# Split weights in the three standing places: all written 64 bytes further on

## The chip, the cores and the metric

The kernel runs on one core of a Trainium2 chip. The metric is the device time of one execution, in microseconds (us). Matrix products are TensorE's (PE in the profile; PEld is its loading of the operand that stays in the array). VectorE (DVE) and ScalarE (ACT) work element by element, GpSimd (POOL) does very little here, and SyncE (SP) issues nearly all DMAs from the device memory into the on-chip buffer, in which a tile has 128 partitions and a free dimension.

## The reference

Two layers of a diffusion backbone over 256 latent tokens of width 2048, with 256 context tokens, everything in float32. Layer 0 projects with one wide matrix into attention heads (q, k, v, a gate) and into a state-space branch (z, x, B, C, dt); layer 1 is a gated short convolution. Cut to the products that matter:

```python
def na_ssd_mixer(h, hc, w_in, ..., w_out, update_ctx):
    p = h @ w_in                      # q, gate, z, k, v, x, B, C, dt
    pc = hc @ w_in[:, base:]          # context: k, v, x, B, C, dt
    ...
    out = jnp.concatenate([ya, yb], axis=-1) @ w_out

def short_conv_mixer(h, w_in, conv_w, w_out):
    p = h @ w_in
    bg, cg, hv, g = jnp.split(p, 4, axis=-1)
    y = bg * dw_conv(cg * hv, conv_w)
    return (jax.nn.silu(g) * y) @ w_out

def reference(x, c, ctx, c_ctx, ada_w, ada_b, norm_g, ...):
    for i in range(DEPTH):
        shift, scale, gate = adaln(c, ada_w[i], ada_b[i])
        h = modulate(rms_norm(x, norm_g[i]), shift[:, None], scale[:, None])
        ...
        x = x + gate[:, None] * y
    return x
```

## The kernel before

**Products in split form.** A float32 matrix product is made of three products of a reduced type (fp32r). Each factor is split into a high part (the value cast to fp32r) and a low part (the value less its high part), and high x high, high x low and low x high are summed in a bank of the accumulator memory. For the activations these parts stand in tiles hH and hL (or mix, h1, y2 later on).

**How a weight comes in.** The weights are read in 454 chunks of 512 KB. `weight` (L410) puts them into a list in the order of their use. `issue` (L381) starts a DMA on SyncE's queue whenever a raw buffer is free. `split` (L422) takes the next chunk when one of the *places* is free: ScalarE casts it into the high part H (L441), and VectorE subtracts H from the raw chunk into the low part Lo (L448, in `low_part`). `use` (L485) hands H and Lo to the products, and `used` (L498) gives the place back. For the whole of layer 0 there are three standing places, the tiles w0, w1, w2 of 2112 elements a partition (L168). Near the end of the output projection three more are made of tiles that are no longer needed (KL; QT with QL; wH5 with wL5, L425), and they serve in turn with the standing ones for the rest.

**Where in a place.** A chunk has 1024 elements a partition. Most chunks are written to elements 0 to 1023 (H) and 1024 to 2047 (Lo). The chunks of the gates, of z and of C are marked in the set `shifted` when they are listed (L522 to L524), and written 16 elements, that is 64 bytes, further on: 16 to 1039 and 1040 to 2063 (L439). Either way H and Lo lie next to each other. The two dt chunks hold both parts in one half of a place (L431).

**How a product reads a place.** `mm` (L201, its product at L204) multiplies. In `mm_act` (L699) the activations are loaded into the array and 512 columns of H or Lo stream through it: this is how q, k, v, both output projections and the second layer's input are made. In `mm_ws` (L709) 128 columns of H or Lo are loaded and the activations stream: 512 columns wide (latent and context) for B and x, 256 wide (latent only) for the gates, z and C. The opening (`first`, L1086, k-block 0) and the next six blocks (`block`, L981) write these products out in an order and at times set by hand. In the opening `high_terms` (L1225) multiplies with a high part before `low` (L965) and `low_terms` (L1235) deal with its low part.

**What sets the order of the rest.** The program is emitted in one order, and a small planner (`Plan`, L38) keeps a time for every engine while it is emitted. It does so by pieces of tiles: `keys` (L50) maps an operand to units of 128 elements (L55), and for each unit it knows when it was last written and read. From the eighth k-block on, generators for the side work (attention heads, state-space groups, row reductions, output stages) wait in queues. After every few products `pump` (L287) asks `may` (L256) whether the planner's times allow the next step of each, and emits it there. The row reductions of the modulation weights (L842) go by the planner's TensorE clock too (L837). `take` (L190) picks the buffer or bank that the planner saw used longest ago.

Of the kernel before, what the change touches and what calls it, by code (L numbers as in the profile page):

```python
# [17 lines left out]
COL_Q, COL_G, COL_Z, COL_K, COL_V, COL_X = 0, 2048, 4096, 6144, 8192, 10240  # L18
COL_B, COL_C, COL_DT = 12288, 13312, 14336
# [122 lines left out]
def kernel(ctx: ExitStack, tc, x, cx, ada0, w0, adaT, w_in, w_out, sc_in, sc_out, rpb, small, const,  # L142
# [12 lines left out]
    def st(shape, tag, dt=F32, name=None):  # L155
        return sb.tile(list(shape), dt, tag=tag, name=name or tag, bufs=1)
# [9 lines left out]
    free_b = [pj.tile([128, 512], F32, tag=f"bank{k}", name=f"bank{k}", bufs=1) for k in range(8)]  # L166
    free_r = [st([128, 1024], f"raw{k}") for k in range(NRAW)]
    places = [st([128, 2112], f"w{k}", F32R) for k in range(NW)]  # L168
    WH = [t[:, :1024] for t in places]
    WL = [t[:, 1024:2048] for t in places]  # L170
    shifted = set()


    xrow = [st([128, D], "KT", name="x0")]
# [26 lines left out]
    def mm(o, l, r, start, stop):  # L201
        if start:
            bits[o.tensor.name] = o.shape[0] == 128 and o.shape[-1] == 512
        E(T.matmul(o, l, r, start=start, stop=stop, skip_group_check=True))  # L204
# [13 lines left out]
    def spawn(q, gen, tmps=0, halves=0, late=0):  # L218
        q.append(Task(gen, tmps, halves, late))
# [125 lines left out]
    def bank(*full_):  # L345
        if not full_:
            return take(free_b)
        b = min(free_b, key=lambda a: (bits.get(a.tensor.name) is not full_[0], plan.last[a.tensor.name]))
        free_b[:] = [a for a in free_b if a is not b]
        return b  # L350
# [30 lines left out]
    def issue():  # L381

        while (loads or later) and (free_r or (loads and callable(loads[0]))):
            if loads and loads[0] is None:
                if not gate[0]:
                    return
                loads.popleft()
                continue
            if loads and callable(loads[0]):
                loads.popleft()()  # L390
                continue
            if later and (not loads or (ngem[0] < loads[0][7] and len(RAW) - ngem[0] >= 5 - loads[0][7])):
                kind, key, w, r0, nb, c0, n = later.popleft()
                ngem[0] += 1
            elif loads:
                kind, key, w, r0, nb, c0, n, _ = loads.popleft()
            else:
                return
            raw = raw_()
            v = raw[:, :nb * n].rearrange("p (b c) -> p b c", b=nb)  # L400
            if w is ada0 or w is w0 or w is adaT:
                E(DMA.dma_start(raw, w[r0]))
            else:
                E(DMA.dma_start(v, w[r0:r0 + nb * 128, c0:c0 + n].rearrange("(b p) c -> p b c", p=128)))
            RAW[key] = (raw, v)

    nw = [0]
    room = [2]

    def weight(w, r0, nb, c0, n):  # L410
        loads.append(("w", nw[0], w, r0, nb, c0, n, room[0]))
        nw[0] += 1
# [5 lines left out]
    def place():  # L418
        in_use.append(free_w.popleft())
        return in_use[-1]  # L420

    def split():  # L422
        k = pos["split"]
        raw, v = RAW.pop(k)
        nb, n = v.shape[1], v.shape[2]  # L425
        w = place()
        if n == 64:

            while lows:
                low_part()  # L430
            W = WH[w].rearrange("p (b c) -> p b c", b=nb)  # L431
            E(S.copy(W[:, :, :64], v))
            E(V.tensor_tensor(out=W[:, :, 64:], in0=v, in1=W[:, :, :64].bitcast(F32), op=ALU.subtract))
            HL[k] = (W, None)
            pos["split"] += 1
            give_raw(raw)
            issue()
            return
        H, Lo = (places[w][:, 16:1040], places[w][:, 1040:2064]) if k in shifted else (WH[w], WL[w])  # L439
        H, Lo = (t[:, :nb * n].rearrange("p (b c) -> p b c", b=nb) for t in (H, Lo))  # L440
        E(S.copy(H, v))  # L441
        lows.append((k, H, Lo, v, raw))
        pos["split"] += 1

    def low_part():

        k, H, Lo, v, raw = lows.popleft()
        E(V.tensor_tensor(out=Lo, in0=v, in1=H.bitcast(F32), op=ALU.subtract))  # L448
        HL[k] = (H, Lo)
        give_raw(raw)  # L450
        issue()
# [5 lines left out]
    def cast_half(b):  # L457
# [4 lines left out]
        raw, v = RAW[0]  # L462
        E((S.copy, V.tensor_copy)[b](WH[0].rearrange("p (b c) -> p b c", b=2)[:, b], v[:, b]))

    def low_half0(b):

        raw, v = RAW[0]
        H, Lo = (w[0].rearrange("p (b c) -> p b c", b=2) for w in (WH, WL))
        E(V.tensor_tensor(out=Lo[:, b], in0=v[:, b], in1=H[:, b].bitcast(F32), op=ALU.subtract))
# [48 lines left out]
    def q_proj(w, c0, nc_, rows=D):  # L518
        room[0] = 2 if w is w_in and c0 >= COL_K else 1
        nb = 1024 // nc_  # L520
        for r0 in range(0, rows, nb * 128):
            if w is w_in and (COL_G <= c0 < COL_K or COL_C <= c0 < COL_DT):  # L522

                shifted.add(nw[0])  # L524
            weight(w, r0, nb, c0, nc_)

    def give_raw(raw):
        if raw.tensor.name not in once_names and not (started[0] and raw.tensor.name in spare_names):
            free_r.append(raw)
# [80 lines left out]
    for i in (2, 3, 4):  # L610
# [4 lines left out]
    ssd_cols = lambda s: [(w_in, COL_B + s * 256, 256), (w_in, COL_C + s * 256, 256), (w_in, COL_X + s * 512, 512),  # L615
                          (w_in, COL_Z + s * 512, 512)]
    q_proj(w_in, CG(0), 512)
    for r0 in (0, 1024):
        weight(w_in, r0, 8, COL_DT, 64)
    for j_ in ssd_cols(0)[1::2]:  # L620
        q_proj(*j_)
    for a in range(1, 4):
        qk = [(w_in, CQ(a), 512), (w_in, CK(a), 512)]
        gv = [(w_in, CG(a), 512), (w_in, CV(a), 512)][::-1 if a in () else 1]
        for j_ in qk + gv + ssd_cols(a) if a < 3 else qk + ssd_cols(a) + gv:
            q_proj(*j_)
# [333 lines left out]
    def cast(i):  # L960
        if pos["split"] <= i:
            assert pos["split"] == i and free_w and i in RAW, (i, pos, list(free_w), sorted(k for k in RAW if type(k) is int))
            split()
# [122 lines left out]
    def first():  # L1086
# [125 lines left out]
        def k_lat(k, term):  # L1212
            for t in range(2):
                if k == 0 and term == 0:
                    box["K", t] = bank()
                H, Lo = (w[0].rearrange("p (b c) -> p b c", b=2) for w in (WH, WL))
                tt = slice(t * 128, (t + 1) * 128)
# [7 lines left out]
        def high_terms(key, t):  # L1225
            ps = psQ[t] if key == "Q" else bank()
            box[key, t] = ps
            k_ = "KVQ".index(key)
            H = WH[k_].rearrange("p (b c) -> p b c", b=2)
            tt = slice(t * 128, (t + 1) * 128)  # L1230
# [4 lines left out]
        def low_terms(key, t):  # L1235
            k_ = "KVQ".index(key)
            Lo = WL[k_].rearrange("p (b c) -> p b c", b=2)
            tt = slice(t * 128, (t + 1) * 128)
# [45 lines left out]
        def ctx_high(t, k):  # L1284
            tt = slice(t * 128, (t + 1) * 128)
            for key in "KV":
                if k == 0:
                    box[key, t] = bank()
                for w in (WH, WL):
                    mm(box[key, t], hH[k][:, tt], w["KV".index(key)].rearrange("p (b c) -> p b c", b=2)[:, k],  # L1290
# [931 lines left out]
    def turn_gen():  # L2222
        yield when(lambda: n_back[0] >= 11.5 and attn[0] == 32 and ssd_done[0] == 8)
        pt = st([128, 2, 4, 256], "PT", name="late")
        for k in range(2):
            late[4 * k:4 * k + 4] = [pt[:, k, q, :] for q in range(4)]
            pts.append(pt[:, k])
        E(V.scalar_tensor_tensor(out=A1, in0=M1[:, 1], scalar=1.0, in1=P_("g1"), op0=ALU.add, op1=ALU.mult))
        for kp in range(0, KB, 2):
            yield when(lambda: ("x1", kp // 4) in got and (kp < 8 or len(passed) == 4))  # L2230
            yield W_("PE", x1[0][:, kp * 128:(kp + 2) * 128], x1[1][:, kp * 128:(kp + 2) * 128], nb=1)
            pt = bank()
            for b in range(2):
                for t in range(2):
                    turn(pt[:, b * 256 + t * 128:b * 256 + (t + 1) * 128], x1[t][:, (kp + b) * 128:(kp + b + 1) * 128])
            if kp == 14:
                yield when(lambda: ("h1", 7, 0) in got)
            for b in range(2):
                kb = kp + b
                if kp < 8 or kp == 14:  # L2240
                    yield W_("ACT", pt)
                    E(S.activation(late[kb], pt[:, b * 256:(b + 1) * 256], AF.Copy, scale=A1[:, kb:kb + 1]))
                else:

                    held[kb] = pt
                got.add(("turn", kb))
            if kp < 8 or kp == 14:
                give(free_b, pt)
# [131 lines left out]
    for ns in ((0, 512), (1024,), (1536,)):  # L2380
# [41 lines left out]
        if len(ns) == 2:  # L2422
            force(lambda: attn[0] == 32 and not side)
            x1 += [st([128, D], "KT", name="x1a"), st([128, D], "Vt", name="x1b")]
            for H, Lo in ((KL[:, 0:2], KL[:, 2:4]), (QT, QL), (st([128, 4, 256], "gt", F32R, name="wH5"), st([128, 4, 256], "sz", F32R, name="wL5"))):

                free_w.append(len(WH))
                WH.append(H.rearrange("p a b -> p (a b)"))
                WL.append(Lo.rearrange("p a b -> p (a b)"))
            spawn(side, turn_gen())  # L2430
# [106 lines left out]
    for i in range(4):  # L2537
        for part, gen in ((1, cg_gen), (2, hv_gen), (3, gg_gen), (0, bg_gen)):
            ps = banks(2)
            kb0 = 0  # L2540
            if i == 0 and part == 1:
# [3 lines left out]
                for t in range(2):  # L2545
                    for kb in range(8):
# [3 lines left out]
                        H, Lo = ws[kb // 2]  # L2550
# [132 lines left out]
```

## Time and profile before

| | us |
|---|---|
| runs | 1724.03, 1723.19, 1724.82 (median 1724.03) |
| the profiled execution | 1723.43 |
| its span, first to last instruction | 1721.6 |
| TensorE products busy | 1715.5 |
| VectorE busy | 1279.5 |
| ScalarE busy | 823.0 |

A group's line in the profile names the source line, the engine, the operation and the tiles (written <- read, buffer numbers left out), the shape, the count, then the busy time and the mean duration, and the idle time of the engine before it with what ended it. For a product the first tile after the arrow is the one that streams, the second the one that is loaded. Products overlap: each shows about 390 ns for 512 columns, while the next starts well before it ends, so the pace is read from the distance of starts. The granted TensorE clock is 1.00 over the whole span.

### The profile page before, as it was taken

The numbers are of one execution on the slowest core, as the hardware profiler recorded it, in microseconds if no ns is written. First come the engines' busy times: TensorE is split into PE (matmuls) and PEld (weight loads), VectorE is DVE, ScalarE is ACT, GpSimd is POOL, SyncE is SP. The second block draws the span as 40 slices with busy tenths as digits, with TensorE's granted clock in tenths as the row PEclk, the third lists the DMA queues.
The fourth block names the chain that finished last, engine by engine and source line by source line (L and its number), as shares of the span: only waits on it lengthen the run. The fifth ranks groups of instructions, "written<-read, shape, count | busy, mean of one in ns | idle before, by whom it ended". The sixth has DMA issues, their size and how long they took to land.

```text
span 1721.6 us, 24689 instructions
## 1 busy us (share of the span) xinstructions
PE 1715.5 (100%) x9129; PEld 1449.9 (84%) x9129; DVE 1279.5 (74%) x2161; ACT 823.0 (48%) x1450; POOL 34.3 (2%) x28
## 2 busy tenths in 40 slices
PE   9999999999999999999999999999999999999999
PEld 5778899888889889889888898888888888888887
DVE  5699878877886778486877587887667767676754
ACT  6578464434553445244444244655444444444342
POOL 0000010000000000000001000000000000000000
PEclk9999999999999999999999999999999999999999
DMA  9988566456645675754775577767857788787863
GB/s 360 355 293 285 199 195 204 152 178 217 222 144 166 205 230 165 243 173 155 226 227 164 191 214 235 237 214 266 288 190 249 274 270 298 251 288 250 286 213 117
DMA packets 191368, 391.03 MB, mean 227 GB/s; under 512 B 16200, under 2 KB 45960, under 8 KB 190992
## 3 DMA queue, kind: packets, MB, share of 16 engines
q1 hardware_dynamic: 183936, 382.88, 67.2%
q10 hardware_dynamic: 7312, 6.59, 1.2%
q8 instruction: 71, 1.16, 0.3%
q14 instruction: 49, 0.40, 0.1%
HBM read 379.79 MB, written 9.62 MB: 226 GB/s over the span
## 4 chain that ended last, share of the span: by engine, by line
PE 99%; DMA 1%; DVE 0%; issue 0%
PE bank L204 96%; PE bank L209 3%; DMA raw<-in_ada 0%; DMA small<-in_small 0%; DVE tmp L2575 0%; DVE tmp L2578 0%
## 5 line engine op out<-in xcount | busy, mean ns | idle before, releaser
L441 ACT CAST w<-raw 128x1024 fp32r<-128x1024 f32 (+1 forms) x336 | 350.9, 1045 | 477.5 <-PE bank L204 389.2
L448 DVE TENSOR_TENSOR w<-raw,w 128x1024 fp32r<-128x1024 f32 (+1 forms) x336 | 406.9, 1215 | 215.0 <-ACT w L441 212.3
L204 PE MATMUL bank<-hH,w 128*128 128x256 f32 (+1 forms) x2064 | 486.5, 324 | 0.0
L204 PE MATMUL bank<-w,hH 128*128 128x512 f32 x1280 | 402.0, 394 | 0.0
L204 PEld LDWEIGHTS bank<-hH,w 128*128 128x128 f32 x2064 | 345.2, 188 | 32.1 <-issue 1.7
L204 PE MATMUL bank<-hL,w 128*128 128x256 f32 (+1 forms) x1040 | 334.7, 322 | 0.0
L204 PEld LDWEIGHTS bank<-w,hH 128*128 128x128 f32 x1280 | 236.9, 188 | 47.2 <-issue 0.8
L204 PE MATMUL bank<-w,hL 128*128 128x512 f32 x640 | 248.6, 391 | 0.0
L204 PEld LDWEIGHTS bank<-hL,w 128*128 128x128 f32 x1040 | 196.4, 189 | 14.5
L204 PE MATMUL bank<-w,h 128*128 128x512 f32 x768 | 178.5, 390 | 0.0
L204 PEld LDWEIGHTS bank<-w,h 128*128 128x128 f32 x768 | 144.0, 188 | 29.7
L842 DVE CUSTOM_DVE_ANT_0 raw<-raw,csb 128x1024 f32<-128x1024 f32 x128 | 155.3, 1219 | 10.5 <-DMA raw<-in_adaT 10.4
L204 PEld LDWEIGHTS bank<-w,hL 128*128 128x128 f32 x640 | 120.1, 188 | 25.3 <-DVE hL L1123 0.4
L204 PE MATMUL bank<-w,mix 128*128 128x512 f32 x588 | 138.4, 392 | 0.0
L204 PEld LDWEIGHTS bank<-w,mix 128*128 128x128 f32 x588 | 109.5, 188 | 22.0 <-issue 0.2
L204 PE MATMUL bank<-KL,h 128*128 128x512 f32 x264 | 63.6, 389 | 0.0
L1817 DVE SCALAR_TENSOR_TENSOR tmp<-bank,cwh,tmp 128x508 f32<-128x508 f32 (+1 forms) x80 | 59.4, 745 | 1.6
L204 PEld LDWEIGHTS bank<-KL,h 128*128 128x128 f32 x264 | 49.6, 188 | 10.3
L448 DVE TENSOR_TENSOR KL<-raw,KL 128x1024 fp32r<-128x1024 f32 x32 | 39.2, 1224 | 23.5 <-ACT KL L441 23.3
L204 PE MATMUL bank<-QT,h 128*128 128x512 f32 x168 | 55.8, 391 | 0.0
L204 PE MATMUL bank<-wH,h 128*128 128x512 f32 x168 | 55.3, 389 | 0.0
L441 ACT CAST QT<-raw 128x1024 fp32r<-128x1024 f32 x32 | 33.6, 1051 | 41.9 <-PE bank L204 34.5
(343 smaller groups left out, 2077.8 us busy)
## 6 DMA issues: line engine op xcount, KB each, us to landing
raw<-in_w_in SPq DMA_DIRECT2D x188, 512.0 KB, 3.7
raw<-in_adaT SPq DMA_DIRECT2D x128, 512.0 KB, 4.8
raw<-in_sc_in SPq DMA_DIRECT2D x128, 512.0 KB, 4.6
raw<-in_w_out SPq DMA_DIRECT2D x64, 512.0 KB, 4.6
raw<-in_ada SPq DMA_DIRECT2D x39, 512.0 KB, 6.2
raw<-in_sc_out SPq DMA_DIRECT2D x32, 512.0 KB, 4.5
tmp<-dram_csr SPq DMA_DIRECT2D x32, 256.0 KB, 5.8
raw<-in_w SPq DMA_DIRECT2D x15, 512.0 KB, 5.9
```

Source lines behind the costliest of these rows:

```text
L204: E(T.matmul(o, l, r, start=start, stop=stop, skip_group_check=True))
L209: E(T.transpose(o, i, ident if k == 128 else ident[:k, :k]))
L441: E(S.copy(H, v))
L448: E(V.tensor_tensor(out=Lo, in0=v, in1=H.bitcast(F32), op=ALU.subtract))
L842: E(V.tensor_tensor_reduce(out=raw, in0=raw, in1=csb, scale=1.0, scalar=0.0, op0=ALU.mult, op1=ALU.add, accum_out=gp[:, h, m:m + 1]))
L1817: E(V.scalar_tensor_tensor(out=do, in0=di, scalar=cwh[:, 32 * k + ch:32 * k + ch + 1], in1=do, op0=ALU.mult, op1=ALU.add))
```

## The change

The set `shifted` goes, and the views WH and WL of the three standing places themselves begin 16 elements further on. So every chunk that is split into w0, w1 or w2 is written there, the dt chunks and those of the opening too, which use WH and WL directly (`cast_half`, `low_half0`, `high_terms`, `low_terms`, `ctx_high`, `ctx_low`). The three later places, made of other tiles, keep their addresses.

```diff
     places = [st([128, 2112], f"w{k}", F32R) for k in range(NW)]
-    WH = [t[:, :1024] for t in places]
-    WL = [t[:, 1024:2048] for t in places]
-    shifted = set()
+    WH = [t[:, 16:1040] for t in places]
+    WL = [t[:, 1040:2064] for t in places]
...
-        H, Lo = (places[w][:, 16:1040], places[w][:, 1040:2064]) if k in shifted else (WH[w], WL[w])
+        H, Lo = WH[w], WL[w]
         H, Lo = (t[:, :nb * n].rearrange("p (b c) -> p b c", b=nb) for t in (H, Lo))
         E(S.copy(H, v))
...
         for r0 in range(0, rows, nb * 128):
-            if w is w_in and (COL_G <= c0 < COL_K or COL_C <= c0 < COL_DT):
-
-                shifted.add(nw[0])
             weight(w, r0, nb, c0, nc_)
```

## The prediction

> **What bounds the kernel now.** I read the page first: busy times, then the chain that ended last.
>
> ```profile
> span 1721.6 us, 24689 instructions
> PE 1715.5 (100%) x9129; PEld 1449.9 (84%) x9129; DVE 1279.5 (74%) x2161; ACT 823.0 (48%) x1450; POOL 34.3 (2%) x28
> ...
> PE 99%; DMA 1%; DVE 0%; issue 0%
> PE bank L204 96%; PE bank L209 3%; DMA raw<-in_ada 0%; DMA small<-in_small 0%; DVE tmp L2575 0%; DVE tmp L2578 0%
> ```
>
> The chain is TensorE from end to end, 96% of it the product helper at L204. A change that touches no product's pace and makes no product wait cannot move the end. So the questions are two: what a product costs when one of its operands lies 64 bytes further on, and whether the split weights come late anywhere. The second is answered by the view of waits, for the weight loads of TensorE (total us, times, longest):
>
> ```profile
> PEld bank L204 <- issue: 20.1, 70, 0.5
> ...
> PEld bank L204 <- DVE w L448: 0.6, 2, 0.4
> ...
> PEld bank L204 <- ACT w L441: 0.4, 1, 0.4
> ```
>
> In 1,721.6 us, TensorE waited 1.0 us for the two halves of split weights together. The splits have cover to spare.
>
> Which products read the three standing places, and how? In a name like bank<-w,hH the operand that streams through the array stands first and the one that is loaded into it second. The groups of TensorE by shape, over the whole span and, for the last one, over its last 91 us:
>
> ```profile
> L204 PE MATMUL bank<-w,hH 128*128 128x512 f32 x1280 | 402.0, 394 | 0.0
> L204 PE MATMUL bank<-hH,w 128*128 128x512 f32 x784 | 255.1, 394 | 0.0
> L204 PE MATMUL bank<-w,hL 128*128 128x512 f32 x640 | 248.6, 391 | 0.0
> L204 PE MATMUL bank<-hH,w 128*128 128x256 f32 x1280 | 232.8, 282 | 0.0
> L204 PE MATMUL bank<-hL,w 128*128 128x256 f32 x640 | 178.7, 279 | 0.0
> L204 PE MATMUL bank<-w,h 128*128 128x512 f32 x768 | 178.5, 390 | 0.0
> L204 PE MATMUL bank<-hL,w 128*128 128x512 f32 x400 | 156.0, 390 | 0.0
> L204 PE MATMUL bank<-w,mix 128*128 128x512 f32 x588 | 138.4, 392 | 0.0
> ```
>
> ```profile
> L204 PE MATMUL bank<-w,y 128*128 128x512 f32 x180 | 41.7, 390 | 0.0
> ```
>
> The 256-wide products, 1280 + 640 = 1,920, are the gates, z and C: their weights are shifted already and stay where they are. The change reaches two other kinds. **Streamed:** 1280 + 640 + 768 + 588 + 180 = 3,456 products of 512 columns whose moving operand is a split weight (k, v, q, both output projections, the second layer's input). **Loaded:** 784 + 400 = 1,184 products of 512 columns whose weight is the loaded operand (x, B, the two dt chunks).
>
> **Their pace.** The means above include the overlap of neighbours, so the pace is read from starts in the timeline. Four stretches without an interruption (start, duration, group):
>
> ```profile
> 355.01 0.39 PE L204 MATMUL bank<-w,hL 128*128 128x512 f32 x1
> ...
> 358.41 0.39 PE L204 MATMUL bank<-w,hL 128*128 128x512 f32 x1
> ```
>
> ```profile
> 1309.68 4.47 PE L204 MATMUL bank<-w,h 128*128 128x512 f32 x19
> 1313.99 2.88 PE L204 MATMUL bank<-KL,h 128*128 128x512 f32 x12
> 1316.71 0.39 PE L204 MATMUL bank<-QT,h 128*128 128x512 f32 x1
> ```
>
> ```profile
> 541.77 0.28 PE L204 MATMUL bank<-hL,w 128*128 128x256 f32 x1
> ...
> 544.95 0.28 PE L204 MATMUL bank<-hL,w 128*128 128x256 f32 x1
> ```
>
> ```profile
> 653.99 0.28 PE L204 MATMUL bank<-hL,w 128*128 128x256 f32 x1
> ...
> 656.71 0.28 PE L204 MATMUL bank<-hL,w 128*128 128x256 f32 x1
> ```
>
> One hL product comes with each two hH products. From 355.01 to 358.41 are 15 products: 3.40 / 15 = 226.7 ns with streamed weights in a standing place, unshifted. From 1309.68 to 1313.99 are 19: 226.8 ns, another standing place; the 12 that follow stream from KL, a tile that is no standing place: 2.72 / 12 = 226.7 ns. The 256-wide form has two paces, with the same shifted weights: 3.18 / 27 = 117.8 ns near 542 us, 2.72 / 24 = 113.3 ns near 654 us. 113.3 is half of 226.7: the fast pace is one price per streamed column, 0.443 ns, and it is the same whether the loaded weight is shifted (113.3), the streamed weight is not (226.7), or the stream comes from elsewhere (KL). That is the central observation.
>
> **The change part by part.** No instruction is added or removed: the same casts, subtractions and products, the same DMAs into the raw buffers, which don't move. Addresses change, and the planner's bookkeeping.
>
> Streamed weights, 3,456 products: no row shows a stream that begins 64 bytes off. The nearest rows are the three undisturbed paces above, all at 0.443 ns a column. I take 0 ns. Ends kept for the range: below, 117.8 − 113.3 = 4.5 ns saved in each, above, one 64-byte piece more in each, 226.7 / 32 = 7.1 ns (both in the rivals).
>
> Loaded weights, 1,184 products: the load of 128 columns is
>
> ```profile
> L204 PEld LDWEIGHTS bank<-hH,w 128*128 128x128 f32 x2064 | 345.2, 188 | 32.1 <-issue 1.7
> ```
>
> 188 ns, beside a product that occupies the array for 226.7. 38 ns of cover remain, and 1,280 of the 2,064 loads in this row are shifted already. Cost 0; if the cover were gone, at most the 4.5 ns between the two 256-wide paces: 1,184 × 4.5 = 5.3 us.
>
> The splits themselves: ScalarE's cast (L441) and VectorE's subtraction (L448) read raw and write the place. Shifted ones are in the trace: between 541 and 556 us the gates are split, between 1290 and 1600 us the second layer's unshifted weights. Groups of those two windows (count | busy us, mean ns | idle before):
>
> ```profile
> L448 DVE TENSOR_TENSOR w<-raw,w 128x1024 fp32r<-128x1024 f32 x5 | 6.1, 1219 | 2.7 <-ACT w L441 2.7
> L441 ACT CAST w<-raw 128x1024 fp32r<-128x1024 f32 x5 | 5.2, 1048 | 3.7 <-PE bank L204 3.1 <-ACT tmp L1811 0.6
> ```
>
> ```profile
> L448 DVE TENSOR_TENSOR w<-raw,w 128x1024 fp32r<-128x1024 f32 x59 | 71.8, 1223 | 37.4 <-ACT w L441 37.1
> L441 ACT CAST w<-raw 128x1024 fp32r<-128x1024 f32 x58 | 61.1, 1053 | 89.5 <-PE bank L204 50.6 <-DMA raw<-in_sc_in 35.6 <-DVE tmp L2507 2.3
> ```
>
> ```profile
> L441 ACT CAST w<-raw 128x1024 fp32r<-128x1024 f32 (+1 forms) x336 | 350.9, 1045 | 477.5 <-PE bank L204 389.2
> ```
>
> 1,219 against 1,223 ns and 1,048 against 1,053: the shift does nothing to either engine, and both are hidden behind TensorE anyway (74% and 48% busy). Were the cover gone, 5 ns in the 256 splits that are newly shifted (336 in this row less the 80 of the gates, z and C) are 1.3 us. Waits: the high and the low part stay disjoint and adjacent, so no engine has a new wait; a place is refilled, as now, after its last product.
>
> The planner: it keeps times by units of 128 elements (L55). Unshifted, the high part covers units 0 to 7, the low part 8 to 15. Shifted, 0 to 8 and 8 to 16: unit 8 is common. Where a high part is read before its low part is written, which only the opening does (`high_terms` before `low_terms`), the planner now sees an order that the chip doesn't have, and its TensorE clock should run a little later, by less than one such subtraction (1.2 us). The opening and the six blocks after it are in a fixed order. From the eighth block on, `may` and the comparison at L837 decide by that clock, so a few transposes, attention products and row reductions may be issued one product earlier or later. What one such interruption of the product stream costs is seen at one of them:
>
> ```profile
> 336.33 0.93 PE L209 MATMUL bank<-const,tmp 128*128 128x128 f32 x7
> 337.01 0.70 PE L204 MATMUL bank<-w,hH 128*128 128x512 f32 x2
> 337.55 0.40 PE L204 MATMUL bank<-w,hL 128*128 128x512 f32 x1
> 337.78 0.62 PE L204 MATMUL bank<-w,hH 128*128 128x512 f32 x2
> ```
>
> ```profile
> 203 pieces in order of time: start us, us, what
> ```
>
> The two products after it take 0.54 us and not 2 × 0.2267 = 0.45: about 0.1 us. The chain has 203 pieces, so some 100 interruptions, 10 us in all. The interruptions remain; they only change places. I take 0, and keep ± 3.4 us (a third of them joined or broken up) and the other thing that changes with their places: a third of the 1,920 narrow products going from one of its paces to the other, 640 × 4.5 = 2.9 us. Together about 6 us to either side.
>
> **Sum:** 0 + 0 + 0 + 0. The profiled execution took 1,723.43 us (its span 1,721.6 and 1.8 around it). The median of the runs is 1,724.03, 0.6 above. I predict the median: 1,724.0 us.
>
> **The rivals.**
> *The order moves (0.20).* The mechanism and its price are above: 1,718 to 1,730, and it counts as a change only beyond 0.2% (3.4 us, about what a measurement of this kernel can tell from no change). For it: the clock feeds many decisions. Against it: TensorE's waits sum to so little that there is nothing to win but interruptions. Faster 0.09, slower 0.11.
>
> *A collision goes (0.09), faster.* If the loaded and the streamed operand, both on the same 64-byte phase now, got in each other's way in the wide products, the shift would take that away; the price by the two paces is 3,456 × 4.5 = 15.6 us: 1,708. Against it: the wide products run at exactly twice the fast narrow pace, so no such excess is seen in them. The larger form of this rival is that the 0.443 ns per column is itself a loss from the place. The Trainium skill, "TensorE: Matmul & The Clock Gate", section "Wait — 56ns, not 53.3ns?", gives a warm product N / 2.4 GHz and about 2.5 ns, which by estimate is 215.8 ns for 512 columns; by it the sum would be 3,456 × 10.9 = 38 us lower, 1,686. The trace disagrees with that page at 226.7 in every place alike, KL among them, so I give this form 0.03 of the 0.09.
>
> *A stream that begins mid-line costs a line (0.11), slower.* If operands are fetched in pieces of 128 bytes or more, a stream of 2,048 bytes that begins 64 bytes off touches one piece more. Price 7.1 ns × 3,456 = 24.5 us: 1,748. It decides from 3.4 us / 3,456 = 1.0 ns a product. For it: no streamed operand in this trace is known to begin there. Against it: shifted weights are loaded, cast and subtracted at no price.
>
> *The change does less than it says:* in the second layer three of the six places are made of other tiles (KL, QT with QL, wH with wL), which don't move. That only halves the two rivals above there.
>
> **How the numbers follow.** Forecast (no change) 0.60, its own range 1,721 to 1,727. Order 0.20, collision 0.09, line 0.11. The forecast and the order make 0.80: the range is 1,717 to 1,732. Faster 0.09 + 0.09 = 0.18, slower 0.11 + 0.11 = 0.22, same 0.60.
>
> **What would show it.** In the changed profile the stretch of w,h products against the KL,h products after it is a test inside one run: one is shifted, the other not. Equal at 226.7: forecast or order. 222 against 226.7: collision. 234: line. The order shows in the count of pieces of the chain (203 now) and in the busy time of the 256-wide groups. The cast and the subtraction should stay at 1,050 and 1,223 ns. I am wrong if a streamed weight's pace moves by over 1 ns, or if the waits of TensorE for w rise by microseconds.

## The result, and the profile after

The changed kernel takes 1739.53 us (median of 4 runs, 1739.43 to 1739.83), the kernel before 1724.12: a ratio of 1.009 (95% interval 1.0073 to 1.0107), 15.4 us slower. The forecast of no change, 1724.0 with a range from 1717 to 1732, was wrong.

The page of the changed kernel (its lines from L172 on are numbered one lower, those behind the third edit, at the old L522, four lower: L203 is the old L204, L440 and L447 the old L441 and L448):

```profile
span 1738.0 us, 24689 instructions
PE 1731.0 (100%) x9129; PEld 1449.6 (83%) x9129; DVE 1280.1 (74%) x2161; ACT 822.3 (47%) x1450; POOL 34.2 (2%) x28
...
PE bank L203 95%; PE bank L208 3%; DMA raw<-in_ada 0%; DMA small<-in_small 0%; DVE tmp L1813 0%; DVE w L447 0%; ACT w L440 0%; DVE tmp L2571 0%; DVE tmp L2574 0%; ACTq L440 0%
```

The span grew by 16.4 us and the busy time of the products by 15.5. All other engines did the same work in the same time. TensorE's weight loads waited no longer for the split weights (total us, times, longest, in the view of waits):

```profile
PEld bank L203 <- DVE w L447: 0.7, 2, 0.4
PEld bank L203 <- ACT w L440: 0.2, 1, 0.2
```

So nothing comes late; the products themselves became slower. Their groups by shape, those that changed and the narrow ones that didn't:

```profile
L203 PE MATMUL bank<-w,hH 128*128 128x512 f32 x1280 | 404.3, 396 | 0.0
L203 PE MATMUL bank<-hH,w 128*128 128x512 f32 x784 | 259.1, 399 | 0.0
L203 PE MATMUL bank<-w,hL 128*128 128x512 f32 x640 | 250.2, 393 | 0.0
L203 PE MATMUL bank<-hH,w 128*128 128x256 f32 x1280 | 232.9, 281 | 0.2 <-DVE w L447 0.2
...
L203 PE MATMUL bank<-hL,w 128*128 128x512 f32 x400 | 158.0, 395 | 0.0
```

The two groups with the weight as the loaded operand gained 5 ns each in mean duration (394 to 399, 390 to 395), those with the weight as the streamed one 2 ns; the narrow ones nothing. The pace, from starts in the timeline. First the loaded kind, then, in the second layer, a stretch that streams shifted weights and the two that follow it from KL and QT, which are not shifted:

```profile
532.64 0.39 PE L203 MATMUL bank<-hL,w 128*128 128x512 f32 x1
...
539.64 0.39 PE L203 MATMUL bank<-hL,w 128*128 128x512 f32 x1
```

```profile
1302.30 8.42 PE L203 MATMUL bank<-w,h 128*128 128x512 f32 x36
1310.55 2.93 PE L203 MATMUL bank<-KL,h 128*128 128x512 f32 x12
1313.32 0.39 PE L203 MATMUL bank<-QT,h 128*128 128x512 f32 x1
...
1316.04 0.39 PE L203 MATMUL bank<-wH,h 128*128 128x512 f32 x1
```

Loaded: 30 products (one hL in three) in 7.00 us, 233.3 ns. In the kernel before the same 30 products:

```profile
527.17 0.39 PE L204 MATMUL bank<-hL,w 128*128 128x512 f32 x1
...
533.97 0.39 PE L204 MATMUL bank<-hL,w 128*128 128x512 f32 x1
```

6.80 us, 226.7 ns. Streamed: 36 products in 8.25 us, 229.2 ns. The 12 from KL take 2.77 us, 230.8 ns, and the 12 from QT and QL 2.72 us, 226.7 again. The KL products are unshifted and yet not at their old pace. Their distances are uneven, 224 to 236 ns, for the first ten; the last two are at 227 and 226, and the stretch after them keeps that pace. So something of the shifted stretch lasts for some products; what it is no run shows.

Where the 16.4 us went, by the distance from each product's start to the next one's start, summed over all products of a kind in the two traces: 1,184 loaded ones 273.0 to 279.6 us (+6.6), 3,456 streamed ones 793.2 to 801.1 (+7.9), 1,134 wide ones from the three later places 257.6 to 259.1 (+1.5), 1,920 narrow ones 225.9 to 226.3 (+0.4). The sum is the whole difference. And it is not the planner: instruction by instruction, the two programs have the same order on every engine, the same buffers and the same waits. They differ in addresses alone. None of the versions below has another order of instructions either; the two that move one part alone also differ from the kernel before in a few waits (17 and 12 instructions).

### The profile page after: what moved, and what is told of

The parts are those of the page before. It is cut to its first block, busy times and chain, and to the rows that moved or that the text cites. A ratio compares the mean times of both kernels' runs of the same rounds, so it can differ in the third digit from the quotient of the medians.

```text
span 1738.0 us, 24689 instructions
## 1 busy us (share of the span) xinstructions
PE 1731.0 (100%) x9129; PEld 1449.6 (83%) x9129; DVE 1280.1 (74%) x2161; ACT 822.3 (47%) x1450; POOL 34.2 (2%) x28
## 4 chain that ended last, share of the span: by engine, by line
PE 99%; DMA 1%; DVE 0%; ACT 0%; issue 0%; ACTq 0%
PE bank L203 95%; PE bank L208 3%; DMA raw<-in_ada 0%; DMA small<-in_small 0%; DVE tmp L1813 0%; DVE w L447 0%; ACT w L440 0%; DVE tmp L2571 0%; DVE tmp L2574 0%; ACTq L440 0%
## 5 line engine op out<-in xcount | busy, mean ns | idle before, releaser
L440 ACT CAST w<-raw 128x1024 fp32r<-128x1024 f32 (+1 forms) x336 | 350.0, 1043 | 486.6 <-PE bank L203 385.7
L447 DVE TENSOR_TENSOR w<-raw,w 128x1024 fp32r<-128x1024 f32 (+1 forms) x336 | 407.0, 1214 | 224.4 <-ACT w L440 222.0
L203 PE MATMUL bank<-hH,w 128*128 128x256 f32 (+1 forms) x2064 | 490.5, 326 | 0.2 <-DVE w L447 0.2
L203 PE MATMUL bank<-w,hH 128*128 128x512 f32 x1280 | 404.3, 396 | 0.0
L203 PEld LDWEIGHTS bank<-hH,w 128*128 128x128 f32 x2064 | 345.1, 188 | 36.6 <-issue 1.8
L203 PE MATMUL bank<-hL,w 128*128 128x256 f32 (+1 forms) x1040 | 336.5, 324 | 0.0
L203 PEld LDWEIGHTS bank<-w,hH 128*128 128x128 f32 x1280 | 236.9, 188 | 49.5 <-issue 0.8
L203 PE MATMUL bank<-w,hL 128*128 128x512 f32 x640 | 250.2, 393 | 0.0
L203 PEld LDWEIGHTS bank<-hL,w 128*128 128x128 f32 x1040 | 196.0, 188 | 16.6
L203 PE MATMUL bank<-w,h 128*128 128x512 f32 x768 | 180.5, 392 | 0.0
L203 PEld LDWEIGHTS bank<-w,h 128*128 128x128 f32 x768 | 144.0, 188 | 31.7
L203 PEld LDWEIGHTS bank<-w,hL 128*128 128x128 f32 x640 | 120.1, 188 | 26.9 <-DVE hL L1119 0.4
L203 PE MATMUL bank<-w,mix 128*128 128x512 f32 x588 | 139.8, 394 | 0.0
L203 PEld LDWEIGHTS bank<-w,mix 128*128 128x128 f32 x588 | 109.6, 188 | 23.3 <-issue 0.2
L203 PE MATMUL bank<-KL,h 128*128 128x512 f32 x264 | 64.6, 393 | 0.0
L203 PEld LDWEIGHTS bank<-KL,h 128*128 128x128 f32 x264 | 49.6, 188 | 11.4
L447 DVE TENSOR_TENSOR KL<-raw,KL 128x1024 fp32r<-128x1024 f32 x32 | 39.2, 1224 | 25.6 <-ACT KL L440 25.5
L203 PE MATMUL bank<-QT,h 128*128 128x512 f32 x168 | 55.8, 391 | 0.0
L203 PE MATMUL bank<-wH,h 128*128 128x512 f32 x168 | 55.3, 389 | 0.0
L447 DVE TENSOR_TENSOR QL<-raw,QT 128x1024 fp32r<-128x1024 f32 x32 | 39.1, 1223 | 20.5 <-ACT QT L440 20.2
```

## The experiments

Two theories were open. **Phase:** a wide product is slower when the two operands that TensorE reads, the loaded and the streamed one, begin on different phases, that is, with different remainders of their start addresses. **Line:** each operand that begins off a 128-byte boundary costs by itself. Below, the *difference* is where the loaded operand begins less where the streamed one begins, modulo 256 bytes, as the allocated addresses give it. In the kernel before all wide products of split weights have difference 0 (every tile concerned begins 128 bytes past a multiple of 256) and the narrow ones 64. In the changed kernel the loaded kind has 64 and the streamed kind -64, that is 192.

**One part alone: the loaded weights.** In `weight` (L410), marked for the shifted place beside the gates, z and C:

```diff
+        if w is w0 and r0 % 4 == 3 or w is w_in and COL_X <= c0 < COL_DT:
+            shifted.add(nw[0])
         loads.append(("w", nw[0], w, r0, nb, c0, n, room[0]))
```

> Beside the gates, z and C only the weights of x and B are shifted by 64 bytes, which are loaded into the array in 512-wide products; the streamed ones stay. In the changed kernel's trace these 1,184 products start 237.7 (hH, 784 of them) and 233.2 ns (hL, 400) apart on average and not 232.1 and 227.6, 6.6 us in all. Phase theory (a product is slower when its loaded and its streamed operand lie on different 64-byte phases) and line theory (each operand that begins off a 128-byte boundary costs, whatever the other does): both 1730.7. If only streamed operands matter: 1724.

Measured: 1731.29 us against 1724.10, ratio 1.0041 (1.0026 to 1.0056). As expected within 0.6 us. The edit moves 1,152 of the 1,184 products; the 32 of the two dt chunks stay at difference 0.

**The other part alone: the streamed weights**, of the standing places and from the second k-block on.

```diff
+        if w is w0 and r0 % 4 != 3 and r0 > 3 or w is w_in and (c0 < COL_G or COL_K <= c0 < COL_X) or any(w is t for t in (w_out, sc_in, sc_out)):
+            shifted.add(nw[0])
         loads.append(("w", nw[0], w, r0, nb, c0, n, room[0]))
...
-        H, Lo = (places[w][:, 16:1040], places[w][:, 1040:2064]) if k in shifted else (WH[w], WL[w])
+        H, Lo = (places[w][:, 16:1040], places[w][:, 1040:2064]) if k in shifted and w < NW else (WH[w], WL[w])
```

> Beside the gates, z and C only the streamed weights are shifted (k, v, q from the second k-block on, both output projections, the second layer's input), not those of x and B. By the changed kernel's trace the streamed products pay 7.8 us and the products from the other three places, which follow them, 1.4 us: 1733.3 by both theories. If only loaded operands matter: 1724. The two parts together should give the whole: (this - before) + (e1_loaded - before) = 15.4.

Measured: 1733.37, ratio 1.0054 (1.0039 to 1.0069). The parts, 7.2 and 9.3 us, make 16.5, against 15.4 for the whole change; each ratio is known to about 2.6 us, so the two agree. Both kinds pay, each on its own.

**No shift at all.** The two lines that fill `shifted` (L522 to L524) are taken out.

> No weight is shifted, the gates, z and C neither: their 1,920 narrow products have both operands on the same phase. Wide products as in the kernel before. Phase theory: the narrow ones have no reason to be slower, all at 113.3 ns, 8 us gained: 1716. Line theory: the same. If the narrow form has another rule than the wide one, it is slower than 1724: by 4.5 ns each and more, 1733 or above.

Measured: 1731.55, ratio 1.0039 (1.0026 to 1.0053). Slower, against both theories as they stood, and a little less than the third guess of 1733: the narrow products pay 3.6 ns each on average, not 4.5. A stretch of narrow products at difference 0:

```profile
543.88 0.28 PE L204 MATMUL bank<-hL,w 128*128 128x256 f32 x1
...
550.72 0.28 PE L204 MATMUL bank<-hL,w 128*128 128x256 f32 x1
```

From the first to the last, 57 products in 6.84 us: 120.0 ns, and no stretch at 113.3 any more. What is best for a wide product is the worst value tried for a narrow one.

**Wide weights 128 bytes further on**, the gates, z and C at 64 as before.

```diff
-    WH = [t[:, :1024] for t in places]
-    WL = [t[:, 1024:2048] for t in places]
+    WH = [t[:, 32:1056] for t in places]
+    WL = [t[:, 1056:2080] for t in places]
```

> The wide weights lie 128 bytes further on and not 64, the gates, z and C at 64 bytes as in both kernels. Phase theory with a period of 128 bytes and line theory: 1724, every wide product at 226.7 ns. If any displacement costs, or the period is 256 bytes or more: 1735 to 1745.

Measured: 1748.60, ratio 1.0141 (1.0126 to 1.0156): worse than 64 bytes, and above both expectations. The line theory falls in the form that it had, every operand of a wide product being on a 128-byte boundary here.

```profile
532.84 0.40 PE L204 MATMUL bank<-hL,w 128*128 128x512 f32 x1
...
539.82 0.40 PE L204 MATMUL bank<-hL,w 128*128 128x512 f32 x1
...
1307.34 8.55 PE L204 MATMUL bank<-w,h 128*128 128x512 f32 x36
1315.73 2.90 PE L204 MATMUL bank<-KL,h 128*128 128x512 f32 x12
```

Loaded 6.98 / 30 = 232.7 ns, streamed 8.39 / 36 = 233.1 ns. At difference 128 both kinds pay nearly the same, which fits a period of 256: 128 and -128 are the same modulo 256.

**The activations moved**, the kernel before otherwise: one empty tile of 64 bytes ahead of the activations' tiles (before L660).

```diff
+    st([128, 16], "pad")
     xnT = [st([128, 512], ("Bl", "Cl")[kb] if kb < 2 else f"hL{kb}", name=f"xm{kb}") for kb in range(KB)]
```

> The kernel before, with 64 empty bytes put ahead of the activations' tiles: all activations (hH, hL, mix, h1, y2) begin 64 bytes off, the wide weights don't, the gates, z and C do. Phase theory: all wide products have unlike phases, those from the three later places too: 1724 + 15.4 + about 1,100 x 3 ns = 1742, plus what e3_none shows for narrow products of like phase. Line theory: the activations are off in every product, wide and narrow: 1742 and above.

Measured: 1760.23 against 1725.42, ratio 1.0203 (1.0188 to 1.0219). Not one weight of the wide products lies elsewhere than before, and this is the slowest kernel of all.

```profile
534.87 0.39 PE L204 MATMUL bank<-hL,w 128*128 128x512 f32 x1
...
541.73 0.39 PE L204 MATMUL bank<-hL,w 128*128 128x512 f32 x1
...
1314.21 8.56 PE L204 MATMUL bank<-w,h 128*128 128x512 f32 x36
1322.61 2.96 PE L204 MATMUL bank<-KL,h 128*128 128x512 f32 x12
1325.41 0.40 PE L204 MATMUL bank<-QT,h 128*128 128x512 f32 x1
```

Loaded, now at difference 192, 6.86 / 30 = 228.7 ns; streamed, now at 64, 8.40 / 36 = 233.3; KL, also at 64, 2.80 / 12 = 233.3. The phase theory, with some 7 us for the narrow products, gave about 1750. The 10 us more come from the sign of the difference: by the sums of starts the streamed products, now at 64, pay 20.4 us and not the 7.9 of the changed kernel, and those from the later places 7.4 and not 3.3, while the loaded ones, now at 192, pay 2.4 and not 6.6. As a time the run doesn't part the theories, since the line theory asked for 1742 and above.

**Both moved**: the changed kernel with the same empty tile. All operands of the products from the standing places are off by 64 bytes, alike.

> The changed kernel, with the same 64 empty bytes: activations and all weights of the standing places begin 64 bytes off, so their phases are alike again; only the three later places differ (about 1,100 products x 3 ns = 3.3 us). This is the run that parts the theories. Phase theory: the wide products are back at 226.7 ns, 1724 + 3.3 = 1727, plus what e3_none shows for narrow products of like phase. Line theory: both operands are off, 1739 or more.

Measured: 1739.72, ratio 1.0083 (1.0068 to 1.0098). As a time this looks like the line theory, and like the changed kernel's 1739.53; the trace says the opposite.

```profile
531.86 0.39 PE L203 MATMUL bank<-hL,w 128*128 128x512 f32 x1
...
538.66 0.39 PE L203 MATMUL bank<-hL,w 128*128 128x512 f32 x1
...
1300.22 8.34 PE L203 MATMUL bank<-w,h 128*128 128x512 f32 x36
1308.40 2.96 PE L203 MATMUL bank<-KL,h 128*128 128x512 f32 x12
1311.20 0.39 PE L203 MATMUL bank<-QT,h 128*128 128x512 f32 x1
```

Loaded 6.80 / 30 = 226.7 ns: fully back. Streamed 8.18 / 36 = 227.2, with the excess in the first five behind other products at difference 64; the 31 after them run at 226.7. The stretch from KL, unshifted against shifted activations, now takes 2.80 / 12 = 233.3. By sums of starts against the kernel before: loaded +0.5 us, streamed +1.4, the 1,134 from the later places +7.4 (6.5 ns each where 3 were allowed for), the narrow ones, now at difference 0, +6.8 as without any shift. These make 16.1 us of the span's 17.1. That the total came out as in the changed kernel is chance: what the wide products of the standing places get back, about 12.6 us, the narrow ones and those of the later places lose. A line theory can't give 226.7 with both operands off.

**All weights 192 bytes further on** (16:1040 becomes 48:1072, and so on).

> The changed kernel with 192 bytes and not 64, for all weights of the standing places. Period of 128 bytes: the same as the changed kernel, 1739.5. A longer period (256 bytes): another time, between 1724 and 1755.

Measured: 1750.62, ratio 1.0148 (1.0131 to 1.0165): not the changed kernel's time, so the period isn't 128 bytes.

```profile
534.09 0.39 PE L203 MATMUL bank<-hL,w 128*128 128x512 f32 x1
...
540.96 0.39 PE L203 MATMUL bank<-hL,w 128*128 128x512 f32 x1
...
1310.18 8.56 PE L203 MATMUL bank<-w,h 128*128 128x512 f32 x36
1318.58 2.90 PE L203 MATMUL bank<-KL,h 128*128 128x512 f32 x12
```

Loaded 6.87 / 30 = 229.0, streamed 8.40 / 36 = 233.3. Against the changed kernel (233.3 and 229.2) the two kinds have changed places, as they must if the sign of the difference counts: loaded now has 192, streamed 64.

**All weights 32 bytes further on** (8:1032).

> The changed kernel with 32 bytes and not 64. If 64-byte pieces alternate between two places that collide: 32 bytes off costs something between nothing and the full price, 1724 to 1745 (narrow products included). If an operand must begin on a 64-byte boundary: more than 1745.

Measured: 1755.80, ratio 1.0177 (1.0162 to 1.0192): above the first range, and inside the second.

```profile
535.12 0.40 PE L203 MATMUL bank<-hL,w 128*128 128x512 f32 x1
...
542.12 0.40 PE L203 MATMUL bank<-hL,w 128*128 128x512 f32 x1
...
1313.96 8.57 PE L203 MATMUL bank<-w,h 128*128 128x512 f32 x36
1322.36 2.92 PE L203 MATMUL bank<-KL,h 128*128 128x512 f32 x12
```

Loaded (difference 32) 7.00 / 30 and streamed (-32, that is 224) 8.40 / 36 are both 233.3 ns. Half of the displacement costs the loaded kind as much as the whole, and the streamed kind more (229.2 at 192). A rule that an operand must begin on a 64-byte boundary isn't needed for it: the wide products pay the same 233.3 with every operand on one, at difference 64.

**Wide weights 256 bytes further on** (64:1088), the narrow ones at 64: the test of the period.

> The wide weights lie 256 bytes further on, the gates, z and C at 64 bytes. Phase theory as it stands now (the difference between the beginnings of the loaded and the streamed operand decides, with a period of 256 bytes): the same time as the kernel before, within 0.1%, wide products at 226.7 ns, although every wide weight is displaced. If only an undisplaced place is fast, or the period is 512 bytes: 1735 to 1755.

Measured: 1724.87 against 1724.11, ratio 1.0002 (0.9993 to 1.0011).

```profile
1307.73 8.32 PE L204 MATMUL bank<-w,h 128*128 128x512 f32 x36
1315.89 2.88 PE L204 MATMUL bank<-KL,h 128*128 128x512 f32 x12
```

8.16 / 36 = 226.7 ns. Every wide weight is displaced by four times as much as in the change, and nothing is lost.

**Other places for the gates, z and C**, in the kernel before (L439: 32:1056, 24:1048 and 20:1044 in place of 16:1040), looking for a faster kernel as well.

> The kernel before with the gates, z and C at 128 bytes and not 64. Known for the narrow products by difference: 0 bytes 121.2 ns on average, 32 bytes 119.8, 64 bytes 117.7, 192 bytes 118.9. If 64 is the best: about 118.5 ns, 1725 to 1727. If the best lies half a period away, all narrow products at 113.3: 1716.

> The kernel before with the gates, z and C at 96 bytes. If the narrow pace changes smoothly with the difference, about as at 64 and 128 bytes: 1722 to 1727. If it goes by 64-byte pieces, an odd 32 bytes costs as at 32: 1728.

> The kernel before with the gates, z and C at 80 bytes, a try for a faster place. Between 64 bytes (117.7 ns on average, 1724.1) and 96 (119.7, 1728.3) by a straight line: 118.7 ns, 1726. If the interrupted stretches settle at 113.3 ns more often than at 64 bytes: 1718 to 1722.

Measured: 1729.32 (ratio 1.0034, 1.0022 to 1.0047), 1728.27 (1.0022, 1.0012 to 1.0031) and 1728.21 (1.0025, 1.0015 to 1.0035). All are slower than 64 bytes. At 128 and at 80 bytes the times lie above both guesses; at 96 the second guess, 1728, came out, though only as a time. No version tried beats the kernel before.

Together, wide products by difference, in the undisturbed stretches used above (36 streamed, 30 loaded products):

| difference | loaded weight, ns | streamed weight, ns |
|---|---|---|
| 0 (before; both moved; 256 bytes) | 226.7 | 226.7 to 227.2 |
| 32 | 233.3 | |
| 64 | 233.3 (changed kernel) | 233.3 (activations moved; 192 bytes further on) |
| 128 | 232.7 | 233.1 |
| 192 | 228.7 (activations moved); 229.0 (192 bytes further on) | 229.2, in other stretches 233.3 (changed kernel) |
| 224 | | 233.3 (32 bytes further on) |

Two differences were reached in two ways, with the operands at other addresses, and cost the same: over all starts, streamed weights at 64 take 235.4 ns with the activations moved and 235.5 with the weights 192 bytes on (229.5 before), loaded weights at 192 take 232.7 in both (230.6 before).

Narrow products, the mean over all 1,920 starts of a trace: 121.2 ns at 0, 119.8 at 32, 117.7 at 64 (kernel before), 120.1 at 80, 119.7 at 96, 120.6 at 128, 118.9 at 192.

## Why the prediction was wrong

*What bounds the kernel; the splits; the waits.* Right. The chain stayed TensorE's, cast and subtraction kept their durations (1,043 and 1,214 ns over the whole page, 1,045 and 1,215 before), and TensorE waited no longer for split weights.

*The planner and the rival "the order moves" (0.20).* Not borne out: not one instruction changed place, although units are shared as described. Whether the planner's clock ran later in the opening no run shows; its decisions were the same.

*"Streamed weights, 3,456 products: I take 0 ns."* This step failed. They pay 2.3 ns on average by the sums of starts (7.9 us), inside the bounds that were kept (-4.5 to 7.1) but not at the value taken, and past the 1 ns that the prediction named as its sign of being wrong.

*"Loaded weights, 1,184 products: cost 0, 38 ns of cover remain."* This failed too, and with it its bound of 4.5: they pay 6.6 us, 5.6 ns each. The load's duration of 188 ns did not change and stayed hidden. So a hidden load isn't a free one: where its operand begins, relative to the streamed one, sets the pace. That its reads slow the product that streams meanwhile or next would explain this, but no run shows it.

*The reasoning under both:* "the same whether the loaded weight is shifted (113.3), the streamed weight is not (226.7), or the stream comes from elsewhere (KL)". The three stretches differed in two things at once. Those at 226.7 were all wide with difference 0; the one at 113.3 was narrow with difference 64. From these no statement about a wide product with another difference follows, and among the products of split weights there was none. The only 512-wide ones of this type at another difference were 32 attention products (P streaming, VH loaded, difference 224), which stand singly between others: all but one have the next start 228 to 236 ns later. No undisturbed pace can be read from these. The run without any shift shows that width and difference act together: 0 is best for the wide, worst for the narrow form.

*The rivals.* "A collision goes, faster" named the right pair, loaded against streamed operand, with the wrong sign: in wide products like phases are the fast ones. That a collision is the cause no run shows. "A stream that begins mid-line costs a line, slower" had the side right and the mechanism wrong: a stream may begin 64 bytes off at no price if the loaded operand does so too (226.7 to 227.2 with both moved). "The change does less than it says" held in the main: the later places return to 226.7 after a few products, and pay 1.5 us in all.

*The test inside one run* worked, but not as put: the KL products after a shifted stretch run at 230.8 ns, slower than the 229.2 of the shifted ones. QT's 226.7 is the clean comparison.

What stays open: why a difference of 192 bytes costs about 2.4 ns where 32, 64, 128 and 224 cost 6 or more; and why a streamed stretch at that difference can hold another pace. Near 205 us in the changed kernel 24 products take 5.60 us, 233.3 ns, where the second layer's take 229.2:

```profile
204.84 0.40 PE L203 MATMUL bank<-w,hL 128*128 128x512 f32 x1
...
210.44 0.40 PE L203 MATMUL bank<-w,hL 128*128 128x512 f32 x1
```

There the loaded operands change in another order (`rows_`, L863, against `mm_act`). That is not the reason: in the run with the streamed weights alone the same 24 products, at the same addresses and in the same order, take 5.49 us, 228.9 ns.

```profile
204.23 0.39 PE L204 MATMUL bank<-w,hL 128*128 128x512 f32 x1
...
209.72 0.39 PE L204 MATMUL bank<-w,hL 128*128 128x512 f32 x1
```

So a difference of 192 has two paces, as the narrow products have at 64 (113.3 and 117.8). Between these two runs only the places of x, B, dt and the first k-block's weights differ, and a few waits. So what ran before the stretch is left as the cause; how it acts no run shows.

## What to carry to other kernels

When TensorE bounds a kernel of such products, the start addresses of the two operands of each product are a tuning parameter, here of up to 3% in pace (226.7 to 233.3 ns), and in this kernel it is their difference modulo 256 bytes that counts, not either alone: an empty tile put ahead of one of them changes it. Wide and narrow products may want different differences, so a placement that helps one form must be tried on the other before it is given to all. And a trace in which all products of a form have the same difference can't tell what another would cost: what was measured on one form is no row for the other.

## What the runs showed of the hardware

Loaded and streamed operand of TensorE are not independent in this kernel: with all else equal, 512-column products start 226.7 ns apart at difference 0 and up to 233.3 ns otherwise, with a period of 256 bytes as far as the runs go (1724.87 against 1724.11 us at a full period). The Trainium skill, "TensorE: Matmul & The Clock Gate", section "Step-by-step: what each phase is for", describes two independent read ports, one for the streamed operand and one for the load. If the two never met, no difference of addresses would matter; the runs disagree with that, at up to 6.6 ns a product. The difference doesn't fix the pace alone: at 192 the same products ran at 228.9 and at 233.3 ns in two runs. Where in the memory or in the engine the two operands meet, no run here shows.
